# A decoder layer in fp32: a third weight pair by seven block products in the gate and up blocks, with the residual kept in DRAM meanwhile

## The chip, the cores and the metric

The kernel runs on one core of a Trainium2 chip. That core has a matmul engine (TensorE, PE), three engines for elementwise work (VectorE or DVE, ScalarE or ACT, GpSimd or POOL), a queue engine (SyncE, SP) that here issues almost all transfers, and 16 DMA engines. Engines run their instructions in order and wait for each other by semaphores.

The metric is the device time of one execution in microseconds (us), the median of several runs. Lower is better.

## The reference

One layer (DEPTH = 1) of a decoder over 256 tokens of 2048 features, all in float32:

```python
mem_n = rmsnorm(mem, mem_norm)
h = x
h = h + hybrid_mixer(rmsnorm(h, norm_mix), w_in, ..., w_out)
h = h + memory_cross_attention(rmsnorm(h, norm_xa), mem_n, w_q, w_k, w_v, w_o)
h = h + swiglu(rmsnorm(h, norm_ffn), w_gate, w_up, w_down)
return rmsnorm(h, norm_final)

def swiglu(h, w_gate, w_up, w_down):
    return (jax.nn.silu(h @ w_gate) * (h @ w_up)) @ w_down
```

The change touches the last step alone: `w_gate` and `w_up` are 2048 x 5632, `w_down` is 5632 x 2048. Mixer and attention stay as they are.

## The kernel before

**Products.** Every float32 operand of a large matmul is split into a high part that PE takes as it is (type `fp32r`) and the rest, a low part. A product is then three matmuls of 128 x 128 by 128 x 512 into one PSUM accumulator: high by high, low activations by high weights, high activations by low weights (`tok_mm`, lines 310, 311, 314). The stationary operand is a block of activations (128 features of 128 tokens), the moving one 512 columns of weights. For the 256 tokens there are two accumulators, called `tb` 0 and 1.

**Weights.** The weights come in one stream of tiles, 128 x 1024, each with two feature blocks of 512 columns (512 KB). `load_to` issues the loads on SP (line 197), up to six tiles ahead, into a pool `raw` of 6. `split_to` makes the high part on ACT (line 236, pool `hi` of 4) and the low part on DVE (line 237, pool `lo` of 4). A plain tile takes 12 matmuls: two feature blocks, two token blocks, three matmuls.

**Gate and up.** The stage runs in 11 blocks of 512 columns, `n` = 0 to 10. In each, gate (`g`) and up (`u`) have eight tiles, `c` = 0 to 7. Four PSUM accumulators (pool `acc` of 4) hold the block: gate and up by two token blocks.

**Seven products.** A gate tile and an up tile of the same features are, with the two token blocks and two feature blocks, a product of 2 x 2 blocks: eight block products the plain way, of three matmuls each, 24. In the blocks in `SEVEN` (1 to 8) the first two such pairs are computed by seven products instead (a Winograd form), 21 matmuls (`seven_mm`, lines 972 to 985). It needs:

- sums of weight blocks: `pair_sums` makes four sums of 128 x 512 on DVE (lines 211 to 214) when the pair's second tile is split, and splits three of them into high and low parts (ACT line 218, DVE line 219), in six tiles of the pool `slots` of 63;
- sums of activation blocks, once for the whole stage: `token_sums`, called in block 0, held in `tmp` tiles (8, all taken by two pairs) in `seven_a`;
- four more PSUM tiles (pool `msc` of 4), `shared[n]`, that collect products used in more than one result. After the block's last pair `p_post` (lines 936 to 940) makes four combinations of them, and `whole` (line 1207) adds one to each accumulator when it is read: for gate in `g_post`, for up in `u_post`.

**End of a block.** `u_post` multiplies gate and up (line 1224), transposes the result in 32 x 32 blocks (line 329), writes it to DRAM (`put`, line 342), reads it back with features on the partitions (`get`, line 349) and splits it into `gs` (lines 1234, 1235), two slots a feature pair, 44 by the end of the stage. The next block's matmuls need the up accumulators free.

**Down.** The down stage computes four blocks of 512 output columns, two at a time, with pairs by seven products too (`down_units`). It adds the residual `res` (8 slots of 128 x 512, loaded from x, updated by the mixer and the attention stage), which stays in SBUF all the while. `load_gain` loads `norm_final` ahead of some down tiles.

**Order.** The order on PE and SP is the order of the code (`manual_schedule`): `ffn_units` and `down_units` list the units, `unit` issues loads and splits ahead of the matmuls of its parts, and generators in `procs` (the `_post` functions) are moved on one step with each unit. On DVE and ACT a scheduler sets the order ahead of time; there is no choice at run time. Functions in `before` are called just before the load of a given weight tile is issued, so what they issue stands ahead of that load in SP's queue.

Of the kernel before, what the change touches and what calls it, by code (L numbers as in the profile page):

```python
# [17 lines left out]
F32 = mybir.dt.float32  # L18
F32R = mybir.dt.float32r
AF = mybir.ActivationFunctionType  # L20
ALU = mybir.AluOpType
# [3 lines left out]
T = 256  # L25
# [2 lines left out]
FF = 5632  # L28
FT = FF // 128
FN = FF // 512  # L30
SEVEN = range(1, 9)
OUT_GAPS = (2, 5, 4, 5)
GAPS = (2, 4, 5, 4, 5, 4)
H = 32
# [38 lines left out]
def ffn_units():  # L73


    o = [[((m, 0, c),)] for h in range(2) for m in "gu" for c in range(4 * h, 4 * h + 4)]
    for n in range(1, FN):
        if n in SEVEN:
            for q, rest in ((0, "g2 g3 g4 u2 u3 u4"), (1, "g5 g6 g7 u5 u6 u7")):
                o.append([(("g", n, q), ("u", n, q))])  # L80
                k = [(a[0], n, int(a[1])) for a in rest.split()]
                o += [[(a,), (b,)] for a, b in zip(k[0::2], k[1::2])]
        else:
            o += [[((m, n, c),), ((m, n, c + 1),)] for m in "gu" for c in range(0, KT // 2, 2)]
    return o
# [34 lines left out]
def stream_plan():  # L120

    p = [(("a0",), 512), (("b0",), 512)]
    p += [(("ab", kt), 1024) for kt in range(1, KT)]
    for n in range(2, 22):
        p += [(("in", n, c), 1024) for c in range(KT // 2)]
    p += [(("wo", n, c), 1024) for n, c in out_order()]
    p += [(k, 1024) for k in order_of(out_units())]
    p += [((m, c), 1024) for m in "kqv" for c in range(KT // 2)]
    p += [(("o", n, c), 1024) for n in range(4) for c in range(2)]
    p += [(k, 1024) for k in order_of(ffn_units() + down_units())]  # L130
    return p


def trunk(tc, wst, vecs, xp, xtp, mp, mtp, wdt_in, nfin, outp):
    nc = tc.nc
    plan = stream_plan()
    index = {k: i for i, (k, _) in enumerate(plan)}
    offs, o = [], 0
# [5 lines left out]
    with ExitStack() as ctx:  # L144
# [12 lines left out]
        drp = E(tc.tile_pool(name="scr", bufs=1, space=DRAM))  # L157
# [5 lines left out]
        def nm(s):  # L163
            cnt[0] += 1
            return f"{s}{cnt[0]}"

        def slot(shape=(128, 512), dt=F32):
            return sp.tile(list(shape), dt, tag="s", name=nm("s"))
# [4 lines left out]
        def acc():  # L173
            return accp.tile([128, 512], F32, tag="a", name=nm("a"))
# [6 lines left out]
        tt = nc.vector.tensor_tensor  # L181
# [87 lines left out]
        def small(name):  # L269
            return cp.tile([128, 2], F32, tag=name, name=nm(name), bufs=4)  # L270
# [15 lines left out]
        def inv_rms(e, n):  # L286
            r = small("rr")
            with tc.high_priority():
                ts(e, e, 1.0 / n, EPS, ALU.mult, ALU.add)
                gtt(r, e, half[:, 0:2], op=ALU.pow)  # L290
            return r
# [63 lines left out]
        procs = []  # L355
# [68 lines left out]
        def ahead_of(i, f):  # L424
            before.setdefault(i, []).append(f)
# [437 lines left out]
        res = [[None] * 4 for _ in range(2)]  # L863
# [9 lines left out]
        def add_to_res(n, accs, sums):  # L873

            for tb in range(2):
                h = res[tb][n]
                tt(h, accs[tb], h, ALU.add)
                j = gtp.tile([128, 512], F32, tag="g", name=nm("j"))
                act(j, h, AF.Square, accum_out=sums[:, tb, n:n + 1])
# [11 lines left out]
        def wait(k):  # L891
            for _ in range(k):
                yield

        def to_features(n, gain, dst, steps=(1, 1, 1)):

            if steps is None:
                for i in range(2):  # L900
                    ps = msc()
                    for f in (2 * i, 2 * i + 1):
                        for tb in range(2):
                            nc.tensor.transpose(ps[:, (f % 2) * T + tb * 128:(f % 2) * T + tb * 128 + 128],
                                                res[tb][n][:, f * 128:f * 128 + 128], ident)
                    for f in (2 * i, 2 * i + 1):
                        dst[4 * n + f] = gained(ps[:, (f % 2) * T:(f % 2) * T + T], gain, 4 * n + f)
                return
            t = turn_blocks([res[tb][n] for tb in range(2)])
            yield from wait(steps[0])  # L910
            w = put(t)
            yield from wait(steps[1])
            d = get(w)
            yield from wait(steps[2])
            for f in range(4):
                dst[4 * n + f] = gained(d[:, f], gain, 4 * n + f)

        def token_scale(name, sums, factor=None):

            e = small("rv")  # L920
            with tc.high_priority():
                nc.vector.tensor_reduce(e, sums, axis=mybir.AxisListType.X, op=ALU.add)
            r = inv_rms(e, D)
            out = cp.tile([128, 2], F32, name=name)
            ts(out, r, 1.0 if factor is None else factor, None, ALU.mult)
            return out


        shared, seven_a = {}, {}
# [19 lines left out]
            return  # L949
            yield  # L950

        def token_sums(key, parts):


            xy = fp.tile([128, 1024], F32, tag="f", name=nm("f"))
            w = 512 // len(parts)
            for i, (hi, lo) in enumerate(parts):
                tt(xy[:, i * w:i * w + w], hi.bitcast(F32), lo.bitcast(F32), ALU.add)
            a11, a21, a12, a22, *o = [xy[:, i * 128:i * 128 + 128] for i in range(8)]
            tt(o[0], a21, a22, ALU.subtract)  # L960
            tt(o[1], a11, o[0], ALU.subtract)
            tt(o[2], a21, a11, ALU.subtract)
            tt(o[3], a12, o[1], ALU.subtract)
            seven_a[key] = []
            for i in range(2):
                h, l = [tp.tile([128, T], F32R, tag="t", name=nm("t")) for _ in range(2)]
                y = xy[:, 512 + i * T:512 + i * T + T]
                nc.scalar.copy(h, y)
                tt(l, y, h.bitcast(F32), ALU.subtract)
                seven_a[key] += [(h[:, j * 128:j * 128 + 128], l[:, j * 128:j * 128 + 128]) for j in range(2)]  # L970
# [71 lines left out]
        for i, parts in enumerate(units_o):  # L1042
            for j in (i, i + 1, i + 2):
                if j < len(units_o) and len(units_o[j][0]) == 2 and units_o[j][0][0] not in seven_a:
                    c = units_o[j][0][0][2]
# [6 lines left out]
            _, n, c = keys[0]  # L1052
# [90 lines left out]
        h2g = {}  # L1143
        h2s = cp.tile([128, 2, 4], F32, name="h2s")
        ff = {}

        def o_post(n, accs):
            add_to_res(n, accs, h2s)
            if n == 3:
                ff["r"] = token_scale("fscale", h2s)  # L1150
            if n == 0:
                yield
            yield from to_features(n, "nffn", h2g, None if n == 0 else (4, 1, 0) if n == 1 else (6, 2, 1))
# [23 lines left out]
        with tc.high_priority():  # L1177
            for mb in range(2):
                Vs.append(slot())
                c = scales["mem"][:, mb:mb + 1]  # L1180
# [21 lines left out]
        def whole(m, n, tb, ps):  # L1202

            if n not in SEVEN:
                return ps
# [34 lines left out]
        def part_mm(part):  # L1240
            m, n, c = part[0]
            if len(part) == 2:
                g, u, p = faccs["g", n], faccs["u", n], shared[n]
                seven_mm(part, side_blocks(h2g, 2 * c), seven_a[c], g, u, p,
                         p + [g[0], g[1], u[0]] if c == 0 else [], p if c == 1 else [])
                return
            start = c == 0
            if n in SEVEN:
                start = (1,) if (m, c) == ("u", 2) else False
            tok_mm(faccs[m, n], part[0], side_blocks(h2g, 2 * c), (0, 1), start, c == KT // 2 - 1)  # L1250

        for i, parts in enumerate(ffn_units()):
            if i == len(ffn_units()) - 3:
                token_sums(("d", 0, 0), [gs[0]])
            if i == 8:
                for c in range(2):
                    token_sums(c, [(h2g[2 * c + k][:, 0:T], h2g[2 * c + k][:, T:]) for k in range(2)])
            post = []
            for part in parts:
                m, n, c = part[0]  # L1260
                for k in part:
                    if k[2] == 0:
                        faccs[k[:2]] = [acc(), acc()]
                if len(part) == 2:
                    if c == 0:
                        shared[n] = [msc() for _ in range(4)]
                    else:
                        post.append(p_post(n, shared[n]))
                elif c == KT // 2 - 1:
                    post.append((g_post if m == "g" else u_post)(n, faccs[m, n]))  # L1270
            unit([(list(part), lambda part=part: part_mm(part)) for part in parts], post or None)
# [123 lines left out]
        for i, parts in enumerate(units):  # L1395
# [7 lines left out]
            if len(parts[0]) == 2:  # L1403
                _, n, c = keys[0]
# [4 lines left out]
            n = keys[-1][1]  # L1409
# [136 lines left out]
```

## Time and profile before

| | |
|---|---|
| median of 3 runs | 1488.6 us (1488.46 to 1488.66) |
| span of the profiled execution, first to last instruction | 1487.0 us |
| DMA packets' bytes | 346.71 MB, mean 233 GB/s |
| weight loads (line 197) | 535 of 512 KB, 4.6 us from issue to landing |
| `put` and `get` | 42 each, 512 KB, 3.3 and 4.9 us |
| low parts of weights on DVE (line 237) | 539, 650.7 us busy |
| high parts of weights on ACT (line 236) | 539, 562.2 us busy |
| low parts of the weight sums (line 219) | 96, 65.0 us busy |

The page gives busy time by engine, then the chain of work that ended last: from the last instruction back, at each step to what released it. An engine that is busy all the time and holds that chain sets the time. A wait of another engine costs nothing by itself. In rows of instructions "out<-in" are the program's tile names without their numbers: `r` raw weights, `h` and `l` their parts, `b` and `f` sums, `s` slots, `a` and `m` PSUM tiles, `g` gate results. The busy time of an engine that overlaps its own instructions is the union of them, so the mean of one can be longer than the distance of two.

### The profile page before, as it was taken

Reading aid. Unit: us, or ns where it says so; the run is one execution under the profiler, and the core shown is the slowest. Engines: PE = TensorE matmul, PEld = TensorE weight load, DVE = VectorE, ACT = ScalarE, POOL = GpSimd, SP = SyncE. Lnnn points to the kernel's source line nnn. Section 1 sums busy time; section 2 is a strip of 40 time slices with the busy share of each in tenths; the row PEclk is TensorE's granted clock in tenths of the full one; section 3 lists DMA queues with packets and bytes.
Section 4 is the critical chain, followed back from the end, with each engine's and each line's share of the span. In section 5 each row is a group of like instructions: output and inputs, shape, how many; then the busy total and the mean of one; then the engine's idle time right before and its main releaser. Section 6 shows DMA issues by size and latency. Waiting matters only on the chain.

```text
span 1487.0 us, 18685 instructions
## 1 busy us (share of the span) xinstructions
PE 1476.3 (99%) x6637; PEld 1216.9 (82%) x6637; DVE 1138.9 (77%) x1596; ACT 837.1 (56%) x1176; POOL 33.8 (2%) x46
## 2 busy tenths in 40 slices
PE   9999999999999999999999999999999999999997
PEld 7788888888888888888888888888888888888886
DVE  6677777776785775997577888888887667979975
ACT  7576654867654554665465555555554444655553
POOL 0001000101000000000000000000000000000000
PEclk9999999999999999999999999999999999999999
DMA  9886766868767675768747676665667665765553
GB/s 361 275 282 227 268 225 219 289 225 308 235 214 278 212 233 198 267 228 283 265 159 237 234 248 212 231 213 206 232 226 245 223 225 198 240 215 196 201 189 108
DMA packets 149214, 346.71 MB, mean 233 GB/s; under 512 B 11360, under 2 KB 62976, under 8 KB 149120
## 3 DMA queue, kind: packets, MB, share of 16 engines
q1 hardware_dynamic: 140064, 338.64, 65.6%
q10 hardware_dynamic: 9056, 6.87, 1.5%
q8 instruction: 52, 0.85, 0.2%
q14 instruction: 42, 0.34, 0.1%
HBM read 321.30 MB, written 24.17 MB: 232 GB/s over the span
## 4 chain that ended last, share of the span: by engine, by line
PE 98%; DMA 0%; issue 0%; SPq 0%; ACT 0%; DVE 0%; DVEq 0%; POOLq 0%; POOL 0%
PE a L310 28%; PE a L311 28%; PE a L314 28%; PE m L985 2%; PE m L983 2%; PE m L982 2%; PE a L982 1%; PE a L985 1%; PE a L983 1%; PE m L731 1%; PE m L314 0%; PE m L310 0%; PE m L311 0%; DMA r<-in_w_dram 0%; PE m L1139 0%
## 5 line engine op out<-in xcount | busy, mean ns | idle before, releaser
L237 DVE TENSOR_TENSOR l<-r,h 128x1024 fp32r<-128x1024 f32 (+1 forms) x539 | 650.7, 1215 | 231.3 <-ACT h L236 220.3
L236 ACT CAST h<-r 128x1024 fp32r<-128x1024 f32 (+1 forms) x539 | 562.2, 1047 | 468.4 <-PE a L311 310.2
L310 PE MATMUL a<-h,s 128*128 128x512 f32 x1855 | 726.3, 392 | 0.4 <-ACT h L236 0.4
L311 PE MATMUL a<-h,s 128*128 128x512 f32 x1855 | 722.5, 389 | 0.0
L314 PE MATMUL a<-l,s 128*128 128x512 f32 x1855 | 498.9, 389 | 0.0
L310 PEld LDWEIGHTS a<-h,s 128*128 128x128 f32 x1855 | 348.5, 188 | 74.7 <-issue 2.0
L314 PEld LDWEIGHTS a<-l,s 128*128 128x128 f32 x1855 | 348.4, 188 | 72.5
L311 PEld LDWEIGHTS a<-h,s 128*128 128x128 f32 x1855 | 348.6, 188 | 71.5
L218 ACT CAST s<-b 128x512 fp32r<-128x512 f32 x64 | 38.7, 616 | 23.5 <-DVE b L211 19.8
L329 DVE STREAM_TRANSPOSE b<-s 128x512 f32<-128x512 f32 x62 | 40.7, 689 | 6.4 <-ACT s L336 6.4
L219 DVE TENSOR_TENSOR s<-b,s 128x512 fp32r<-128x512 f32 x64 | 43.2, 683 | 0.0
L672 DVE SCALAR_TENSOR_TENSOR t<-t,vec,t 128x255 f32<-128x255 f32 (+2 forms) x72 | 33.1, 490 | 3.9 <-ACT t L669 3.2
L211 DVE TENSOR_TENSOR b<-r,r 128x512 f32<-128x512 f32 x32 | 21.9, 685 | 14.3 <-DMA r<-in_w_dram 14.2
L336 ACT ACTIVATE s<-a,xr 128x512 f32<-128x512 f32 x42 | 26.4, 679 | 3.6 <-PE a L314 3.6
L1207 DVE TENSOR_TENSOR f<-a,f 128x512 f32<-128x512 f32 x32 | 20.5, 683 | 8.5 <-PE a L314 8.4
L985 PE MATMUL m<-s,t 128*128 128x512 f32 x64 | 24.9, 389 | 0.0
L982 PE MATMUL m<-s,t 128*128 128x512 f32 x64 | 24.9, 389 | 0.0
L983 PE MATMUL m<-s,t 128*128 128x512 f32 x64 | 24.9, 389 | 0.0
L218 ACT CAST s<-r 128x512 fp32r<-128x512 f32 x32 | 19.8, 617 | 6.0 <-DVE r L214 5.9
L212 DVE TENSOR_TENSOR r<-r 128x512 f32<-128x512 f32 x32 | 22.0, 686 | 0.4
L1234 ACT CAST s<-f 128x512 fp32r<-128x512 f32 x22 | 13.5, 619 | 15.4 <-DMA f<-w 15.4
L219 DVE TENSOR_TENSOR s<-r,s 128x512 fp32r<-128x512 f32 x32 | 21.8, 683 | 0.4 <-ACT s L218 0.4
(232 smaller groups left out, 1058.2 us busy)
## 6 DMA issues: line engine op xcount, KB each, us to landing
r<-in_w_dram SPq DMA_DIRECT2D x535, 512.0 KB, 4.6
w<-b SPq DMA_DIRECT2D x42, 512.0 KB, 3.3
f<-w SPq DMA_DIRECT2D x42, 512.0 KB, 4.9
s<-acsT ACTq DMA_DIRECT2D x24, 256.0 KB, 5.3
s<-in_xt_dram SPq DMA_DIRECT2D x16, 256.0 KB, 6.6
s<-in_mt_dram SPq DMA_DIRECT2D x8, 256.0 KB, 6.1
s<-in_m_dram SPq DMA_DIRECT2D x8, 256.0 KB, 5.9
s<-in_x_dram SPq DMA_DIRECT2D x7, 256.0 KB, 7.4
```

The source lines that it names most:

```text
L218: nc.scalar.copy(h, x)
L219: tt(l, x, h.bitcast(F32), ALU.subtract)
L236: nc.scalar.copy(h[:, c], r[:, c])
L237: tt(l[:, c], r[:, c], h[:, c].bitcast(F32), ALU.subtract)
L310: mm(ps[tb], ah, h[:, w], start=first and i == ks[0], stop=False)
L311: mm(ps[tb], al, h[:, w], start=False, stop=False)
L314: mm(ps[tb], blocks(i, tb)[0], l[:, i * 512:i * 512 + 512], start=False, stop=stop and i == ks[-1])
L329: nc.vector.transpose(t[:, tb * 512:tb * 512 + 512], src[tb])
L672: stt(a[:, d:], u[:, 0:T - d], v("cw", 4 * ct + k), a[:, d:], ALU.mult, ALU.add)
L982: mm(ps, ah, bh, start=any(ps is q for q in start), stop=False)
L983: mm(ps, al, bh, start=False, stop=False)
L985: mm(ps, ah, bl, start=False, stop=any(ps is q for q in stop))
```

## The change

In blocks 1 to 9 three pairs go by seven products, in block 10 two; before it was two in blocks 1 to 8. With three pairs the tiles stand in the order pair, `g3 g4 u3`, pair, `g5 u4 g6`, pair, `g7 u5 u6 u7`. The third pair's token sums take two slots instead of `tmp` tiles. The residual is written to DRAM in block 0 (`park`), its eight slots are free in between, and it is read back (`unpark`) ahead of the down tiles ("d", 0, 10) to ("d", 0, 17).

```diff
-SEVEN = range(1, 9)
+SEVEN = {n: 3 if n < 10 else 2 for n in range(1, 11)}
...
         if n in SEVEN:
-            for q, rest in ((0, "g2 g3 g4 u2 u3 u4"), (1, "g5 g6 g7 u5 u6 u7")):
+            plan = {2: ("g2 g3 g4 u2 u3 u4", "g5 g6 g7 u5 u6 u7"),
+                    3: ("g3 g4 u3", "g5 u4 g6", "g7 u5 u6 u7")}[SEVEN[n]]
+            for q, rest in enumerate(plan):
                 o.append([(("g", n, q), ("u", n, q))])
                 k = [(a[0], n, int(a[1])) for a in rest.split()]
-                o += [[(a,), (b,)] for a, b in zip(k[0::2], k[1::2])]
+                o += [[(a,) for a in k[i:i + 2]] for i in range(0, len(k), 2)]
...
-        def token_sums(key, parts):
+        def token_sums(key, parts, wide=False):
...
+            if wide:
+                h, l = slot(dt=F32R), slot(dt=F32R)
+                nc.scalar.copy(h, xy[:, 512:])
+                tt(l, xy[:, 512:], h.bitcast(F32), ALU.subtract)
+                seven_a[key] = [(h[:, j * 128:j * 128 + 128], l[:, j * 128:j * 128 + 128]) for j in range(4)]
+                return
...
+        parked = drp.tile([2, 4, 128, 512], F32, name="parked")
+
+        def park(n):
+
+            yield from wait(12)
+            for tb in range(2):
+                nc.sync.dma_start(parked[tb, n], res[tb][n])
+                yield
+
+        def unpark(tb, n):
+            res[tb][n] = slot()
+            nc.sync.dma_start(res[tb][n], parked[tb, n])
+
+        for n in range(4):
+            for tb in range(2):
+                ahead_of(index[("d", 0, 10 + 2 * n + tb)], lambda tb=tb, n=n: unpark(tb, n))
...
+            procs.append(park(n))
...
-                         p + [g[0], g[1], u[0]] if c == 0 else [], p if c == 1 else [])
+                         p + [g[0], g[1], u[0]] if c == 0 else [], p if c == SEVEN[n] - 1 else [])
...
-                start = (1,) if (m, c) == ("u", 2) else False
+                start = (1,) if (m, c) == ("u", SEVEN[n]) else False
...
-                for c in range(2):
-                    token_sums(c, [(h2g[2 * c + k][:, 0:T], h2g[2 * c + k][:, T:]) for k in range(2)])
+                for c in range(3):
+                    token_sums(c, [(h2g[2 * c + k][:, 0:T], h2g[2 * c + k][:, T:]) for k in range(2)], c == 2)
...
-                    else:
+                    elif c == SEVEN[n] - 1:
                         post.append(p_post(n, shared[n]))
```

Lines of the changed kernel are 2 higher up to 953, and 25 higher from the gate and up stage on: 237 becomes 239, 211 to 214 become 213 to 216, 219 becomes 221, 937 becomes 939, 1207 becomes 1232, 1224 becomes 1249, 1235 becomes 1260.

The order on DVE just after the end of block 1, before: it begins with the last transpose of `u_post`; then come the splits of plain tiles (237) and the sums of block 2's second pair (211 to 214), with the two splits of the returned result (1235) between them.

```order
L329 STREAM_TRANSPOSE b_7867<-g_7790 128x512
L237 TENSOR_TENSOR l_7875<-r_7773,h_7874 128x1024
L237 TENSOR_TENSOR l_7897<-r_7830,h_7896 128x1024
L237 TENSOR_TENSOR l_7901<-r_7840,h_7900 128x1024
L237 TENSOR_TENSOR l_7935<-r_7878,h_7934 128x1024
L211 TENSOR_TENSOR b_7982<-r_7916,r_7918 128x512
L237 TENSOR_TENSOR l_7939<-r_7880,h_7938 128x1024
L212 TENSOR_TENSOR r_7918<-r_7918 128x512
L1235 TENSOR_TENSOR s_7971<-f_7932,s_7970 128x512
L213 TENSOR_TENSOR b_7982<-b_7982,r_7918 128x512
L237 TENSOR_TENSOR l_7979<-r_7916,h_7978 128x1024
L1235 TENSOR_TENSOR s_7975<-f_7932,s_7974 128x512
```

And in the changed kernel, from the same transpose:

```order
L331 STREAM_TRANSPOSE b_7901<-g_7824 128x512
L239 TENSOR_TENSOR l_7909<-r_7807,h_7908 128x1024
L239 TENSOR_TENSOR l_7931<-r_7864,h_7930 128x1024
L239 TENSOR_TENSOR l_7935<-r_7874,h_7934 128x1024
L213 TENSOR_TENSOR b_7966<-r_7874,r_7912 128x512
L214 TENSOR_TENSOR r_7912<-r_7912 128x512
L215 TENSOR_TENSOR b_7966<-b_7966,r_7912 128x512
L221 TENSOR_TENSOR s_7972<-b_7966,s_7971 128x512
L216 TENSOR_TENSOR r_7874<-b_7966,r_7874 128x512
L221 TENSOR_TENSOR s_7976<-b_7966,s_7975 128x512
L239 TENSOR_TENSOR l_7984<-r_7912,h_7983 128x1024
L221 TENSOR_TENSOR s_7980<-r_7874,s_7979 128x512
```

The second pair's sums now follow two plain splits and the split of the pair's own first tile, and their splits (221) follow at once; the returned result's splits come after them.

The order on DVE at the end of block 10 and the start of the down stage, before: `u_post` of block 10 (1224, 329), then the sums and splits of the first down pair.

```order
L1224 SCALAR_TENSOR_TENSOR g_10801<-a_10785,fscale,g_10801 128x512
L1224 SCALAR_TENSOR_TENSOR g_10803<-a_10786,fscale,g_10803 128x512
L329 STREAM_TRANSPOSE b_10972<-g_10801 128x512
L329 STREAM_TRANSPOSE b_10972<-g_10803 128x512
L211 TENSOR_TENSOR b_10979<-r_10911,r_10913 128x512
L212 TENSOR_TENSOR r_10913<-r_10913 128x512
L213 TENSOR_TENSOR b_10979<-b_10979,r_10913 128x512
L219 TENSOR_TENSOR s_10985<-b_10979,s_10984 128x512
L214 TENSOR_TENSOR r_10911<-b_10979,r_10911 128x512
L219 TENSOR_TENSOR s_10989<-b_10979,s_10988 128x512
L237 TENSOR_TENSOR l_10997<-r_10913,h_10996 128x1024
L219 TENSOR_TENSOR s_10993<-r_10911,s_10992 128x512
```

And in the changed kernel:

```order
L1232 TENSOR_TENSOR f_11073<-a_10828,f_11073 128x512
L1232 TENSOR_TENSOR f_11073<-a_10829,f_11073 128x512
L1249 SCALAR_TENSOR_TENSOR g_11151<-f_11073,fscale,g_11151 128x512
L1249 SCALAR_TENSOR_TENSOR g_11154<-f_11073,fscale,g_11154 128x512
L331 STREAM_TRANSPOSE b_11204<-g_11151 128x512
L331 STREAM_TRANSPOSE b_11204<-g_11154 128x512
L213 TENSOR_TENSOR b_11211<-r_11135,r_11137 128x512
L214 TENSOR_TENSOR r_11137<-r_11137 128x512
L215 TENSOR_TENSOR b_11211<-b_11211,r_11137 128x512
L221 TENSOR_TENSOR s_11217<-b_11211,s_11216 128x512
L216 TENSOR_TENSOR r_11135<-b_11211,r_11135 128x512
L221 TENSOR_TENSOR s_11221<-b_11211,s_11220 128x512
```

The two corrections of the up accumulators (1232) are new there, ahead of the same rows, so that these rows end two places short: the split of the pair's second tile, next to last in the rows before, is the row that follows.

SP's queue around block 10's `put` and `get` (342, 349), before: loads of down tiles (197) and of `norm_final` (1281).

```order
L1281 DMA s_10954<-in_nfin_dram 128x512
L197 DMA r_10956<-in_w_dram 128x1024
L197 DMA r_11012<-in_w_dram 128x1024
L1281 DMA s_11020<-in_nfin_dram 128x512
L197 DMA r_11022<-in_w_dram 128x1024
L342 DMA w_11045<-b_10972 128x2x512
L197 DMA r_11055<-in_w_dram 128x1024
L197 DMA r_11071<-in_w_dram 128x1024
L349 DMA f_11085<-w_11045 128x8x128
```

And in the changed kernel, where these lines are 344, 351, 199 and 1306:

```order
L1306 DMA s_11184<-in_nfin_dram 128x512
L199 DMA r_11186<-in_w_dram 128x1024
L1165 DMA s_11244<-parked 128x512
L199 DMA r_11246<-in_w_dram 128x1024
L1165 DMA s_11254<-parked 128x512
L1306 DMA s_11256<-in_nfin_dram 128x512
L199 DMA r_11258<-in_w_dram 128x1024
L344 DMA w_11281<-b_11204 128x2x512
L199 DMA r_11291<-in_w_dram 128x1024
L199 DMA r_11307<-in_w_dram 128x1024
L351 DMA f_11321<-w_11281 128x8x128
```

Two loads of the parked residual (1165) now stand ahead of down tiles there; the other six follow in the same way behind the `get`.

## The prediction

> **What bounds the kernel now.** I read the page first, then busy time by windows, groups of instructions, waits, and the order of time in one gate/up block. Line numbers are those of the kernel before.
>
> ```profile
> span 1487.0 us, 18685 instructions
> PE 1476.3 (99%) x6637; PEld 1216.9 (82%) x6637; DVE 1138.9 (77%) x1596; ACT 837.1 (56%) x1176; POOL 33.8 (2%) x46
> PE 98%; DMA 0%; issue 0%; SPq 0%; ACT 0%; DVE 0%; DVEq 0%; POOLq 0%; POOL 0%
> ```
>
> TensorE (PE) is busy 1476.3 of 1487.0 us and holds 98% of the chain that ended last. So time goes where matmuls go, as long as no other engine makes PE wait. The runs' median is 1488.6 us, so 1.6 us lie around the span; I add them to every result below.
>
> ```profile
> 920.00:960.00 40.00, 40.00 (x178) 33.15 (x177) 33.90 (x43) 21.50 (x26) 0.00 (x0) 1.00 0.62 216
> 1160.00:1200.00 40.00, 40.00 (x178) 33.15 (x177) 23.16 (x23) 17.36 (x19) 0.00 (x0) 1.00 0.65 224
> 1240.00:1280.00 40.00, 40.00 (x178) 33.06 (x177) 35.45 (x55) 21.18 (x27) 0.00 (x0) 1.00 0.69 230
> 1360.00:1400.00 40.00, 40.00 (x178) 33.15 (x177) 38.88 (x67) 24.22 (x34) 0.00 (x0) 1.00 0.56 188
> ```
>
> Columns: length, then PE, PEld, DVE, ACT, POOL busy, granted clock, DMA share, GB/s. PE has no gap in any of these and its clock is 1.00. VectorE (DVE) is busy 33.90 of 40 us in blocks with two pairs (first row), 23.16 in plain blocks (second), and once 38.88 of 40, in the down stage, with PE still full. ScalarE is half idle everywhere. The next engine that could bind is therefore DVE, and only in the gate/up blocks that the change loads further.
>
> **What the change removes.** The period of a two-pair block stands between two equal places of the program, the up evacuations of neighbouring blocks:
>
> ```profile
> 907.01 1.29 DVE L1207 TENSOR_TENSOR f<-a,f 128x512 f32<-128x512 f32 x2 [1.04 <-PE a L314]
> 908.22 1.40 DVE L1224 SCALAR_TENSOR_TENSOR g<-f,fscale,g 128x512 f32<-128x512 f32 x2
> 909.54 1.30 DVE L329 STREAM_TRANSPOSE b<-g 128x512 f32<-128x512 f32 x2
> 910.76 3.45 DVE L237 TENSOR_TENSOR l<-r,h 128x1024 fp32r<-128x1024 f32 x3
> 917.10 0.69 DVE L211 TENSOR_TENSOR b<-r,r 128x512 f32<-128x512 f32 x1 [0.98 <-DMA r<-in_w_dram]
> 918.85 0.68 DVE L212 TENSOR_TENSOR r<-r 128x512 f32<-128x512 f32 x1
> 919.45 0.68 DVE L1235 TENSOR_TENSOR s<-f,s 128x512 fp32r<-128x512 f32 x1
> 920.05 0.68 DVE L213 TENSOR_TENSOR b<-b,r 128x512 f32<-128x512 f32 x1
> 920.65 1.22 DVE L237 TENSOR_TENSOR l<-r,h 128x1024 fp32r<-128x1024 f32 x1
> 921.79 0.68 DVE L1235 TENSOR_TENSOR s<-f,s 128x512 fp32r<-128x512 f32 x1
> 949.17 1.29 DVE L1207 TENSOR_TENSOR f<-a,f 128x512 f32<-128x512 f32 x2 [1.05 <-PE a L314]
> ```
>
> 949.17 - 907.01 = 42.16 us for 12 plain tiles of 12 matmuls and 2 pairs of 21, 186 in all: 0.2267 us a matmul. (A matmul's own 0.39 us overlaps its neighbours and is no price.) A pair of tiles costs 21 matmuls by the seven products and 24 plain, so each new pair takes 3 x 0.2267 = 0.68 us off PE. There are 16 pairs before (8 blocks x 2) and 29 after (9 x 3 + 2), 13 more, and 39 matmuls fewer, as PE's order has it (6433 rows, then 6394). **The gain on PE is 39 x 0.2267 = 8.84 us.** A three-pair block takes 183 x 0.2267 = 41.48 us on PE.
>
> **What it adds to DVE.** Each new pair needs four sums (L211 to L214) and three splits (L219); blocks 9 and 10 also get the four combinations of L937 to L940 and the four corrections of L1207.
>
> ```profile
> L237 DVE TENSOR_TENSOR l<-r,h 128x1024 fp32r<-128x1024 f32 x229 | 276.6, 1217 | 70.8 <-ACT h L236 70.5
> L219 DVE TENSOR_TENSOR s<-b,s 128x512 fp32r<-128x512 f32 x50 | 33.6, 683 | 0.0
> L1207 DVE TENSOR_TENSOR f<-a,f 128x512 f32<-128x512 f32 x32 | 20.5, 683 | 8.5 <-PE a L314 8.4
> L937 DVE TENSOR_TENSOR f<-m,f 128x512 f32<-128x512 f32 x9 | 6.2, 690 | 8.9 <-PE m L985 8.9
> ```
>
> The mean of one is 0.68 us, but the starts show what it occupies: 918.85, 919.45, 920.05, 920.65 are 0.60 apart, and a 1024-wide split takes 1.14 (920.65 to 921.79). I price by starts. A three-pair block holds 16 splits x 1.14 = 18.2, 21 pair operations x 0.60 = 12.6, eight of L937 to L940 and L1207 x 0.605 = 4.8 (907.01 to 908.22 for two), two of L1224 1.32, two transposes 1.22, two of L1235 1.2, and some 0.5 where a sum must wait for the one just ahead: **39.9 us of DVE against 41.48 us of PE**, 96%. That fits only if the waits inside the block shrink to 1.6 us.
>
> ```profile
> DVE l L237 <- ACT h L236: 20.1, 36, 0.9
> DVE b L211 <- DMA r<-in_w_dram: 10.5, 9, 1.6
> DVE f L937 <- PE m L985: 7.8, 7, 1.1
> DVE f L1207 <- PE a L314: 6.3, 6, 1.0
> ```
>
> These are the waits of 310 us (7.4 blocks; total, times, longest). Three of the four are DVE being early: for PE's accumulators (L937, L1207), and for a ScalarE cast that itself waits until PE frees one of four `hi` tiles. They vanish when DVE is later. The fourth, a pair's second weight tile still under way, is 1.4 us a block. In the order before, that load stands behind the store of the previous block in SP's queue; in the new one the loads of the second pair stand ahead of the store, and only the next block's first pair is exposed: its load goes out when the third pair's tiles are split, and DVE has just three splits (3.4 us) to do until it needs it.
>
> ```profile
> r<-in_w_dram SPq DMA_DIRECT2D x114, 512.0 KB, 4.3
> ```
>
> With 4.3 us to land, DVE idles about 1 us there, but the next thing in its queue waits for PE's third pair anyway.
>
> So I walk through one block along DVE's order, from PE's first matmul of the block at 0. PE (2.72 us a plain tile, 4.76 a pair) starts the second pair at 12.9, the third at 25.8, and ends at 41.5. DVE: the previous block's up evacuation (907.01 to 910.76) to 3.75; three splits to 7.2; the second pair's sums and splits to 12.9, of which PE reads the last ones from 15.2; three splits and two of L1235 to 17.5; the third pair's to 24.1, read from 28.1; one split to 25.2. For the next one ScalarE must first cast into a `hi` tile that PE frees at 24.9 (cast done 26.0): DVE waits 0.85. Two splits to 29.0; two sums of the next first pair to 30.4, where PE's third pair has just ended; the combinations, the gate's corrections, the rest of that pair's sums and splits and two plain splits, back to back, to 41.7. The up evacuation thus starts 0.2 us after PE ended the block. What is late next is u's first accumulator: PE needs it 16 matmuls (3.6 us) into the block, DVE frees it after 0.2 + 0.7. **I take no PE stall in the nine blocks**; the other end is rival 1. Below nothing is excluded: the change takes nothing else off PE.
>
> **The change of stage.** Block 10 now has corrections, so two L1207 stand between PE's last up matmul and the sums of the first down pair. Before:
>
> ```profile
> 1247.01 1.41 DVE L1224 SCALAR_TENSOR_TENSOR g<-a,fscale,g 128x512 f32<-128x512 f32 x2 [1.09 <-PE a L314]
> 1249.56 0.65 DVE L211 TENSOR_TENSOR b<-r,r 128x512 f32<-128x512 f32 x1
> 1253.31 1.22 DVE L237 TENSOR_TENSOR l<-r,h 128x1024 fp32r<-128x1024 f32 x1
> 1254.52 0.39 PE L983 MATMUL m<-s,t 128*128 128x512 f32 x1
> 1254.75 0.40 PE L985 MATMUL m<-l,t 128*128 128x512 f32 x1
> ```
>
> DVE works from 1247.01 without a pause; the split that L985 at 1254.75 reads ends at 1254.53. There is no slack at all, so 2 x 0.605 = **1.2 us are a stall of PE**, once. The queue behind it (splits of the next plain tiles) has over 2 us in hand, so it isn't paid twice.
>
> **Parking and the rest.** Eight stores and eight loads of 256 KB join SP's queue.
>
> ```profile
> s<-in_xt_dram SPq DMA_DIRECT2D x16, 256.0 KB, 6.6
> GB/s 361 275 282 227 268 225 219 289 225 308 235 214 278 212 233 198 267 228 283 265 159 237 234 248 212 231 213 206 232 226 245 223 225 198 240 215 196 201 189 108
> ```
>
> The nearest row is the 256 KB loads at the start, 6.6 us to land. The eight loads back move 2.1 MB in the 40 us after block 10, where 230 GB/s move already (the window 1240:1280): 282 in all, under the 361 of the first slice. They wait for slots that PE frees in block 10 or in the first down pair, well before the weight loads behind them are due. I take nothing; the other end is rival 3. The extra token sums for the third pair (about 2 us of DVE, once, in block 0) and block 9's and 10's combinations lie where DVE has 17 us free in 40 (1160:1200), under PE.
>
> **Sum.** 1487.0 - 8.84 + 1.2 = 1479.4 us span, **1481.0 us** with the 1.6 around it.
>
> **Rivals.**
>
> 1. *Waits don't shrink enough.* DVE does 39.9 us of work and keeps 1.4 us for the weight tile and 0.6 for ScalarE: 41.9, 0.4 over PE, in nine blocks 3.8 us, less a reserve of about 1 us before PE feels it: 1484 us. For it: the margin is 4%. Against: 38.88 of 40 us in the down stage with PE full.
>
> 2. *DVE becomes the bound: slower.* If an operation holds DVE for its whole duration, a block is 16 x 1.217 + 21 x 0.683 + 8 x 0.685 + 2 x (0.744 + 0.685 + 0.686), the last three from the rows below, or 43.5 us. That is 2.0 over PE, 18 in nine blocks, less a reserve of 2: 1481.0 + 16 = **1497 us**. It decides from 41.48 us a block, 1.6 over the price by starts: 0.03 us more for each of the 51 operations.
>
> ```profile
> L1224 DVE SCALAR_TENSOR_TENSOR g<-f,fscale,g 128x512 f32<-128x512 f32 x16 | 11.2, 744 | 0.0
> L329 DVE STREAM_TRANSPOSE b<-g 128x512 f32<-128x512 f32 x22 | 14.3, 685 | 0.0
> L1235 DVE TENSOR_TENSOR s<-f,s 128x512 fp32r<-128x512 f32 x22 | 15.0, 686 | 1.8 <-PE a L314 0.9 <-ACT s L1234 0.8
> ```
>
> Against it are the starts 0.60 apart, under the 0.68 of one. The Trainium skill speaks for it: "VectorE: DVE Perf Modes", section Terms, says that the pipeline is flushed after each operation and the next can't issue until it is empty; its section on the TRN2 errata gives (N+151)/0.96, 691 ns for N = 512, which fits the trace's 683 as a duration. By that rule the sum is this rival's; the trace's starts disagree with it as an issue interval.
>
> 3. *The loads back cost what was gained.* If no bandwidth were to spare, 2.1 MB at 230 GB/s delay the down weights by 9 us. Weight tiles are loaded six ahead (6 x 2.72 - 4.3 = 12 us in hand), which would hide it; but a pair's sums need both tiles early. If that leaves 2 us, the cost is 7: 1488 us. The first slice's 361 GB/s speak against it.
>
> That the change doesn't do what it says is excluded by the count of matmuls.
>
> **How the numbers follow.** Forecast 0.68 (from 1479.5, just under the PE sum without the stall, to 1482.5), rival 1 0.14, rival 3 0.08, rival 2 0.10. The range reaches through rival 1: 1479.5 to 1486.0, which leaves out 0.18. A measurement tells about 0.2%, 3 us, from no change: faster (under 1485.6) 0.80, same 0.10, slower 0.10.
>
> **What would show it.** After the change the windows of the gate/up stage show PE 40.00 of 40 with DVE near 38.5; the block period between up evacuations is 41.5 us (42 or more means rival 1, 43.5 rival 2); "L1207 <- PE" waits fall to near nothing; one PE gap of about 1.2 us stands where the first down pair waits for its split; SP shows no long wait at the loads back. PE idle in the middle of the stage, released by DVE, would prove me wrong.

## The result and the profile after

The changed kernel takes **1480.8 us** (median of 4 runs, 1480.44 to 1482.02) against 1488.6 us before: ratio 0.995, 95% interval 0.9936 to 0.9964. That is 7.8 us or 0.5% faster, and the interval does not reach 1. The page of the changed kernel:

```profile
span 1478.7 us, 18815 instructions
PE 1467.5 (99%) x6598; PEld 1209.3 (82%) x6598; DVE 1200.5 (81%) x1710; ACT 858.1 (58%) x1218; POOL 35.8 (2%) x46
PE 98%; DVE 1%; issue 0%; DMA 0%; SPq 0%; ACT 0%; DVEq 0%; POOLq 0%; POOL 0%
```

PE has 39 matmuls fewer (6637 to 6598), DVE 61.6 us more work, and PE still holds 98% of the chain. In busy time by windows of 40 us (length, then PE, PEld, DVE, ACT, POOL, granted clock, DMA share, GB/s) the two gate/up windows of before and the change of stage (the last row) now read:

```profile
920.00:960.00 40.00, 40.00 (x178) 33.14 (x177) 38.98 (x52) 23.05 (x30) 0.00 (x0) 1.00 0.65 233
1160.00:1200.00 40.00, 40.00 (x178) 33.10 (x178) 38.03 (x50) 23.20 (x30) 0.00 (x0) 1.00 0.66 228
1240.00:1280.00 40.00, 39.13 (x173) 32.06 (x173) 39.86 (x65) 23.74 (x32) 0.00 (x0) 1.00 0.71 253
```

DVE is busy 38 to 39 of 40 us and PE shows no hole in the first two windows. The last one has the only hole: 39.13 of 40. The waits of the stage, DVE's in the same 310 us for which the prediction gave them before (total, times, longest):

```profile
DVE l L239 <- ACT h L238: 11.6, 20, 1.5
DVE b L213 <- DMA r<-in_w_dram: 1.4, 2, 0.8
DVE f L1232 <- PE a L316: 0.4, 1, 0.4
```

13.4 us in place of 44.7. All the waits of PE in the whole run are two rows, the first of them at the start as before:

```profile
PE m L446 <- POOL U L442: 1.8, 1, 1.8
PE m L993 <- DVE l L239: 0.9, 1, 0.9
```

The second is the one at the first down pair. In order of time, PE and then DVE there:

```profile
1245.27 0.39 PE L991 MATMUL m<-s,t 128*128 128x512 f32 x1
1246.53 0.50 PE L993 MATMUL m<-l,t 128*128 128x512 f32 x1 [0.87 <-DVE l L239]
1246.86 0.40 PE L993 MATMUL m<-s,t 128*128 128x512 f32 x1
...
1237.76 1.29 DVE L1232 TENSOR_TENSOR f<-a,f 128x512 f32<-128x512 f32 x2 [1.05 <-PE a L316]
1241.51 0.65 DVE L213 TENSOR_TENSOR b<-r,r 128x512 f32<-128x512 f32 x1
1245.25 1.22 DVE L239 TENSOR_TENSOR l<-r,h 128x1024 fp32r<-128x1024 f32 x1
```

DVE works from 1237.76 without a pause to the end of the split at 1246.47, and PE starts the matmul that reads it at 1246.53. By starts PE loses 1.26 - 0.23 = 1.03 us there and 0.34 - 0.23 = 0.11 at the next matmul: 1.14 us.

### The profile page after: what moved, and what is told of

Its sections match the earlier page's. It is cut to its first block, busy times and chain, and to the rows that moved or that the text cites. A ratio compares the mean times of both kernels' runs of the same rounds, so it can differ in the third digit from the quotient of the medians.

```text
span 1478.7 us, 18815 instructions
## 1 busy us (share of the span) xinstructions
PE 1467.5 (99%) x6598; PEld 1209.3 (82%) x6598; DVE 1200.5 (81%) x1710; ACT 858.1 (58%) x1218; POOL 35.8 (2%) x46
## 4 chain that ended last, share of the span: by engine, by line
PE 98%; DVE 1%; issue 0%; DMA 0%; SPq 0%; ACT 0%; DVEq 0%; POOLq 0%; POOL 0%
PE a L312 27%; PE a L313 27%; PE a L316 27%; PE m L993 3%; PE m L990 3%; PE m L991 3%; PE a L991 2%; PE a L990 2%; PE a L993 2%; PE m L733 1%; PE m L316 0%; PE m L313 0%; PE m L312 0%; DMA r<-in_w_dram 0%; PE m L1147 0%
## 5 line engine op out<-in xcount | busy, mean ns | idle before, releaser
L312 PE MATMUL a<-h,s 128*128 128x512 f32 x1751 | 685.7, 392 | 0.1
L313 PE MATMUL a<-h,s 128*128 128x512 f32 x1751 | 681.9, 389 | 0.0
L316 PE MATMUL a<-l,s 128*128 128x512 f32 x1751 | 471.1, 389 | 0.0
L312 PEld LDWEIGHTS a<-h,s 128*128 128x128 f32 x1751 | 329.0, 188 | 70.5 <-issue 2.0
L316 PEld LDWEIGHTS a<-l,s 128*128 128x128 f32 x1751 | 328.7, 188 | 68.5
L313 PEld LDWEIGHTS a<-h,s 128*128 128x128 f32 x1751 | 329.0, 188 | 67.4
L220 ACT CAST s<-b 128x512 fp32r<-128x512 f32 x90 | 55.4, 617 | 54.4 <-DVE b L213 52.3
L221 DVE TENSOR_TENSOR s<-b,s 128x512 fp32r<-128x512 f32 x90 | 61.7, 685 | 0.0
L214 DVE TENSOR_TENSOR r<-r 128x512 f32<-128x512 f32 x45 | 30.9, 688 | 0.8
L216 DVE TENSOR_TENSOR r<-b,r 128x512 f32<-128x512 f32 x45 | 30.8, 684 | 0.2
L221 DVE TENSOR_TENSOR s<-r,s 128x512 fp32r<-128x512 f32 x45 | 30.8, 684 | 0.0
L215 DVE TENSOR_TENSOR b<-b,r 128x512 f32<-128x512 f32 x45 | 30.7, 683 | 0.0
L993 PE MATMUL m<-s,t 128*128 128x512 f32 x72 | 28.0, 389 | 0.0
L991 PE MATMUL m<-s,t 128*128 128x512 f32 x72 | 28.0, 389 | 0.0
L990 PE MATMUL m<-s,t 128*128 128x512 f32 x72 | 28.0, 389 | 0.0
```

The costliest lines, as they stand in the source:

```text
L220: nc.scalar.copy(h, x)
L221: tt(l, x, h.bitcast(F32), ALU.subtract)
L312: mm(ps[tb], ah, h[:, w], start=first and i == ks[0], stop=False)
L313: mm(ps[tb], al, h[:, w], start=False, stop=False)
L316: mm(ps[tb], blocks(i, tb)[0], l[:, i * 512:i * 512 + 512], start=False, stop=stop and i == ks[-1])
L990: mm(ps, ah, bh, start=any(ps is q for q in start), stop=False)
```

## The experiments

Ten kernels ran. Each time stands beside runs of the kernel before on the same chip (1488.3 to 1488.5 us).

| kernel | median, us | ratio to before, 95% interval | expected, us |
|---|---|---|---|
| park_alone | 1488.4 | 0.9998 (0.9989 to 1.0007) | 1488.6 |
| two_pairs | 1487.0 | 0.999 (0.9982 to 0.9999) | 1487.0 |
| plain10 | 1481.1 | 0.995 (0.9938 to 0.9961) | 1481.1 |
| late_pair | 1479.8 | 0.994 (0.9927 to 0.9953) | 1479.7 |
| best | 1479.1 | 0.9937 (0.9925 to 0.995) | 1479.1 |
| dve1 | 1484.1 | 0.997 (0.9959 to 0.9982) | 1480.8 to 1482 |
| dve2 | 1503.7 | 1.0102 (1.0088 to 1.0116) | 1495 |
| four_pairs | 1502.2 | 1.0091 (1.0076 to 1.0106) | 1501 |
| free1 | 1481.5 | 0.9955 (0.9941 to 0.9969) | 1480.8 to 1481.6 |
| free2 | 1497.5 | 1.0061 (1.0048 to 1.0073) | 1497 |

### Parking alone

```diff
-SEVEN = {n: 3 if n < 10 else 2 for n in range(1, 11)}
+SEVEN = {n: 2 for n in range(1, 9)}
...
-                for c in range(3):
+                for c in range(2):
                     token_sums(c, ...
```

> Pairs as before the change (two in blocks 1 to 8), with the residual still parked in DRAM and loaded back. Theory (parking costs nothing): the time of the kernel before, 1488.6 us, within 0.5, and no PE gap over 0.2 us from the gate and up stage on. Rival (the loads back delay the down weights): 1 to 7 us more, as PE gaps in the 40 us after block 10, with DVE or ACT waiting there for weight loads.

The time is that of before within the interval. The waits of PE in the whole run:

```profile
PE m L446 <- POOL U L442: 1.8, 1, 1.8
PE a L312 <- ACT h L238: 1.0, 1, 1.0
```

Both lie in the first 10 us of the program, on the first weights. No wait of PE is left where the residual comes back, so **parking is hidden** and rival 3 falls. In the changed kernel the transfers (the page's DMA issues: number, size, us to landing) and the longest of SP's waits at the loads back (L1165) read:

```profile
parked<-s SPq DMA_DIRECT2D x8, 256.0 KB, 8.0
s<-parked SPq DMA_DIRECT2D x8, 256.0 KB, 6.9
```

```profile
SPq L1165 <- DMA f<-w: 1.2, 1, 1.2
```

The loads land after 6.9 us, near the 6.6 that the prediction took from the first ones of the program, and SP hardly stops at them: its three other waits at L1165 are 0.2 or 0.3 us.

### Two pairs in blocks 1 to 10

```diff
-SEVEN = {n: 3 if n < 10 else 2 for n in range(1, 11)}
+SEVEN = {n: 2 for n in range(1, 11)}
...
-                for c in range(3):
+                for c in range(2):
                     token_sums(c, ...
```

> Two pairs in blocks 1 to 10, no third pair, parking kept: 20 pairs, 12 matmuls fewer than before. Theory (0.2267 us a matmul, and a stall of 1.1 us because block 10 has corrections now): 1488.6 - 2.72 + 1.1 = 1487.0 us, with one PE gap of about 1.1 us at the first down pair. Rival (the stall comes with the third pairs, which leave DVE late): no gap, 1485.9 us.

It takes 1487.0 us, and the waits of PE hold the same row as in the changed kernel:

```profile
PE m L993 <- DVE l L239: 0.9, 1, 0.9
```

There is no third pair here, so the stall does not come from those. Common to both kernels are block 10's two pairs with their corrections, and the loads back; `park_alone` has the loads back too and no such wait.

### Block 10 plain

```diff
-SEVEN = {n: 3 if n < 10 else 2 for n in range(1, 11)}
+SEVEN = {n: 3 for n in range(1, 10)}
```

> Three pairs in blocks 1 to 9, block 10 plain: 27 pairs, 6 matmuls more than the changed kernel. Theory (the stall at the first down pair is the two corrections of block 10): the stall of 1.1 us goes and 6 x 0.2267 = 1.36 us of matmuls come: 1480.8 + 0.25 = 1481.1 us, no PE gap at the first down pair. Rival (the stall has another cause, such as the loads back on SP's queue): the gap stays and the time is 1482.2 us.

It takes 1481.1 us. Of PE's waits only those at the start of the program remain, the 1.8 us as before and

```profile
PE a L312 <- ACT h L238: 0.4, 1, 0.4
```

The loads back stand here as in the changed kernel, so the stall was not theirs. Of the 1.36 us that block 10's two pairs save on PE, its corrections give back 1.14: the change would have lost almost nothing without block 10.

### The first down pair later, and a third pair in block 10

`late_pair`:

```diff
-        for c, k in enumerate(GAPS):
+        for c, k in enumerate(((4,) if n == 0 else GAPS[:1]) + GAPS[1:]):
...
-            before.setdefault(index[("d", 0, 9 + 2 * n)], []).append(lambda n=n: load_gain(n))
+            before.setdefault(index[("d", 0, 10 + 2 * n)], []).append(lambda n=n: load_gain(n))
```

> The changed kernel with the first down pair two plain tiles later (a gap of four tiles in place of two; the loads of norm_final move one tile later with it). Theory (the split that PE waits for is 1.1 us late, and two tiles give 5.4 us): the gap goes, 1480.8 - 1.1 = 1479.7 us. Rival (DVE or the loads are behind by more, and the stall only moves): a PE gap of 0.5 us or more remains somewhere in the first 40 us of the down stage, 1480.3 us or more.

`best` has, besides this:

```diff
-SEVEN = {n: 3 if n < 10 else 2 for n in range(1, 11)}
+SEVEN = {n: 3 for n in range(1, 11)}
```

> late_pair with a third pair in block 10 too: 30 pairs, 3 matmuls fewer. Theory: 3 x 0.2267 = 0.68 us less than late_pair, 1479.1 us, no PE gap. Rival (DVE is too late at the end of block 10 for a third pair there): a PE gap around the first down pair, 1479.8 us or more.

Besides the 1.8 us at the start PE waits once in the whole run of `best`, at the start too:

```profile
PE a L312 <- ACT h L238: 0.2, 1, 0.2
```

The stall is gone in both (`late_pair` waits for the same cast at the start, 0.9 us, and nowhere else). The times fall by 1.0 and a further 0.7 us, as worked out; the ratio's intervals overlap with that of the changed kernel, so it is the missing row that shows the gain, and the times agree with it. `late_pair` moves the loads of `norm_final` as well; that the stall was theirs is excluded by `plain10`, which has them in the old place and no stall. `best` is the fastest of all that ran: 1479.1 us.

### More work for DVE

`dve1` does the first sum of every gate/up pair twice, `dve2` three times; what is computed stays the same.

```diff
-            tt(f[:, a], g[:, a], u[:, a], ALU.add)
+            for _ in range(2 if key[0] == "g" else 1):
+                tt(f[:, a], g[:, a], u[:, a], ALU.add)
```

> The changed kernel with the first sum of each gate/up pair done twice, the same result: 3 more DVE operations of 128x512 in a block of blocks 1 to 9 (2 in block 10). Theory (an operation holds DVE for 0.60 us; DVE's waits of about 1.7 us a block are reserve): 3 x 0.60 = 1.8 us a block use the reserve up and no more: 1480.8 to 1482 us, with DVE's waits for ACT casts in the stage near zero. Rival (the operations take their whole 0.68 us, 2.05 us a block, and the waits are no reserve because they are set by PE): 9 x 1 us or more, 1489 us or more.

> The same with the first sum done three times: 6 more operations in a block. Theory (0.60 us each): 3.6 - 1.75 = 1.85 us a block over PE, 9 blocks 16.6 us, less 2 to 3 us of lead that PE can lose before it waits: 1480.8 + 14 = 1495 us, block period 43.3 us, PE waiting for DVE. Rival by durations (0.683 us each): 4.1 - 1.75 = 2.35 us a block, 21 - 2.5, 1499 us, block period 43.8 us. Rival (DVE has much more hidden slack): below 1485 us.

Both were slower than expected: 3.3 us over the changed kernel in place of 0 to 1.2, and 22.9 in place of 14. In order of time, one block of `dve2` from one `u_post` (L1250) to the next:

```profile
956.20 1.41 DVE L1250 SCALAR_TENSOR_TENSOR g<-f,fscale,g 128x512 f32<-128x512 f32 x2
...
963.25 2.14 DVE L214 TENSOR_TENSOR b<-r,r 128x512 f32<-128x512 f32 x3
965.42 0.69 DVE L215 TENSOR_TENSOR r<-r 128x512 f32<-128x512 f32 x1
966.03 0.69 DVE L216 TENSOR_TENSOR b<-b,r 128x512 f32<-128x512 f32 x1
...
1000.41 1.40 DVE L1250 SCALAR_TENSOR_TENSOR g<-f,fscale,g 128x512 f32<-128x512 f32 x2
```

The period is 44.21 us, and the three equal sums (x3) take 965.42 - 963.25 = 2.17, that is 0.72 each, where the next ones are 0.61 apart. In the program's order on DVE the repeated sum waits, by DVE's own semaphore, for the end of the one ahead, since both write the same place:

```
L214 TENSOR_TENSOR b_7974<-r_7882,r_7920 128x512 [waits DMAHW4_49]
L214 TENSOR_TENSOR b_7974<-r_7882,r_7920 128x512 [waits DVE_49] x2
L215 TENSOR_TENSOR r_7920<-r_7920 128x512 [waits DVE_49]
L216 TENSOR_TENSOR b_7974<-b_7974,r_7920 128x512
```

My expectation priced it like a sum without such a wait. At 0.72, DVE's work of a block without the extra is 44.21 - 6 x 0.72 = 39.9 us, and from `dve1`, whose period is 42.01, 42.01 - 3 x 0.72 = 39.85:

```profile
949.75 1.41 DVE L1250 SCALAR_TENSOR_TENSOR g<-f,fscale,g 128x512 f32<-128x512 f32 x2
991.76 1.41 DVE L1250 SCALAR_TENSOR_TENSOR g<-f,fscale,g 128x512 f32<-128x512 f32 x2
```

To test that reading, `free1` and `free2` add as many sums, which write the half that a later sum overwrites, so that neither has to wait for a sum just ahead. `free1` has the first of the two added places, `free2` both:

```diff
+            if key[0] == "g":
+                tt(f[:, b], g[:, a], u[:, a], ALU.add)
             tt(f[:, a], g[:, a], u[:, a], ALU.add)
+            if key[0] == "g":
+                tt(f[:, b], g[:, a], u[:, a], ALU.add)
```

> The changed kernel with 3 more DVE operations a block again, but none that must wait for the one just ahead: each gate/up pair's first sum is also written to the half of the same buffer that the third sum overwrites. Theory (in dve1 and dve2 the repeated sums stand 0.72 us apart because each waits for the end of the one ahead, which writes the same place; an operation without that wait takes 0.60): block period 39.86 + 1.8 = 41.66 us, 0.18 over PE, 9 x 0.18 = 1.6 us, about the lead that dve1 and dve2 showed: 1480.8 to 1481.6 us. Rival (an added operation costs 0.72 us whatever it is): as dve1, period 42.02, 1484.1 us.

> The same with two such operations for each pair, one ahead of the first sum and one behind it, 6 more a block. Theory: 39.86 + 3.6 = 43.46 us a block, 9 x 1.98 = 17.8 us, less a lead of 1.6: 1497 us. Rival (0.72 us each): as dve2, period 44.2, 1503.7 us. If only the second of the two, which writes the same place two operations later, waits for the end of the one ahead of it: 43.8 us, 1500 us.

Both times came out as the theory has them (1481.5 and 1497.5 us). `free2` in order of time; L214, L215 and L217 are the three sums, L218 the second sum of before:

```profile
954.01 1.40 DVE L1253 SCALAR_TENSOR_TENSOR g<-f,fscale,g 128x512 f32<-128x512 f32 x2
961.05 0.68 DVE L214 TENSOR_TENSOR b<-r,r 128x512 f32<-128x512 f32 x1
961.66 0.68 DVE L215 TENSOR_TENSOR b<-r,r 128x512 f32<-128x512 f32 x1
962.26 0.68 DVE L217 TENSOR_TENSOR b<-r,r 128x512 f32<-128x512 f32 x1
962.98 0.69 DVE L218 TENSOR_TENSOR r<-r 128x512 f32<-128x512 f32 x1
...
997.61 1.41 DVE L1253 SCALAR_TENSOR_TENSOR g<-f,fscale,g 128x512 f32<-128x512 f32 x2
```

0.61, 0.60 and then 0.72 apart: only the second sum, which overwrites what the one ahead still reads, waits. L217, which overwrites what L214 wrote two places ahead, still starts 0.60 after L215. Each of them lasts 0.68 or 0.69 all the same. The period is 43.60. A window of `free1`, and the first matmuls of two later blocks, show how far DVE can be filled:

```profile
920.00:960.00 40.00, 40.00 (x178) 33.12 (x177) 39.90 (x53) 22.18 (x29) 0.00 (x0) 1.00 0.64 226
```

```profile
988.16 0.39 PE L992 MATMUL m<-h,s 128*128 128x512 f32 x1
1029.79 0.39 PE L992 MATMUL m<-h,s 128*128 128x512 f32 x1
```

DVE is busy 39.90 of 40 and PE shows no hole. But the two blocks start 41.63 us apart, 0.15 over the 41.48 of PE's matmuls. PE loses that much a block there, spread so thin that neither its busy time nor its waits show it: a matmul lasts 0.39 us and the next starts 0.23 after it, so one that starts up to 0.16 us late leaves no hole.

### Four pairs

Built on `late_pair`, with the fourth pair's token sums in slots as the third's:

```diff
-SEVEN = {n: 3 if n < 10 else 2 for n in range(1, 11)}
+SEVEN = {n: 4 if n < 10 else 2 for n in range(1, 11)}
...
-                    3: ("g3 g4 u3", "g5 u4 g6", "g7 u5 u6 u7")}[SEVEN[n]]
+                    3: ("g3 g4 u3", "g5 u4 g6", "g7 u5 u6 u7"),
+                    4: ("g4 u4", "g5 u5", "g6 u6", "g7 u7")}[SEVEN[n]]
...
-                for c in range(3):
+                for c in range(4):
```

> late_pair with four pairs in blocks 1 to 9 (order: pair, g4 u4, pair, g5 u5, pair, g6 u6, pair, g7 u7): 27 matmuls fewer than late_pair, 6.1 us on PE, and 7 more DVE operations a block. Theory (DVE becomes the bound): DVE needs 39.9 + 7 x 0.60 = 44.1 us a block, PE 40.8; 9 blocks at 44.1 in place of 41.5 are 23.5 us more, less 2 to 3 of lead: 1479.8 + 21 = 1501 us. Rival (DVE is still not the bound, the gain goes on): 1473.7 us.

The row of `u_post` in neighbouring blocks, and the waits of PE but for the 1.8 us at the start:

```profile
957.27 1.41 DVE L1250 SCALAR_TENSOR_TENSOR g<-f,fscale,g 128x512 f32<-128x512 f32 x2
1001.33 1.40 DVE L1250 SCALAR_TENSOR_TENSOR g<-f,fscale,g 128x512 f32<-128x512 f32 x2
```

```profile
PE a L991 <- DVE f L1233: 13.6, 8, 1.7
PE m L994 <- DVE l L240: 6.9, 8, 0.9
PE a L313 <- ACT s L890: 1.4, 1, 1.4
PE a L314 <- DVE s L891: 0.6, 1, 0.6
```

DVE sets the period, 44.06 us, in place of 41.48, and PE, with 27 matmuls less to do, waits for it in eight of the nine blocks. The last two rows are of block 0, where the fourth pair's token sums get in the way. They cost about 4 us, as the last section works out, which the expectation did not have: that it came near the time is in part luck. The step after the third pair turns the gain into a loss of 22 us, some 18 of them by DVE.

## Why the prediction was right

**The matmuls.** 39 at 0.2267 us. The records of PE are 39 fewer, and the first matmuls of neighbouring three-pair blocks start 41.48 us apart, as predicted (41.47 in the second of these):

```profile
988.23 0.39 PE L990 MATMUL m<-h,s 128*128 128x512 f32 x1
1029.71 0.39 PE L990 MATMUL m<-h,s 128*128 128x512 f32 x1
1071.18 0.39 PE L990 MATMUL m<-h,s 128*128 128x512 f32 x1
```

The prediction wanted this judged by the distance of `u_post` rows, and gave 42 us or more to rival 1. That sign is not safe:

```profile
1031.12 1.40 DVE L1249 SCALAR_TENSOR_TENSOR g<-f,fscale,g 128x512 f32<-128x512 f32 x2
1073.49 1.40 DVE L1249 SCALAR_TENSOR_TENSOR g<-f,fscale,g 128x512 f32<-128x512 f32 x2
1114.07 1.40 DVE L1249 SCALAR_TENSOR_TENSOR g<-f,fscale,g 128x512 f32<-128x512 f32 x2
```

The distances are 42.37 and 40.58 us, while PE goes on at 41.48. In the first of the two blocks DVE waits 0.82 us for a pair's weight tile and is late at its end; in the second its waits for casts are 0.73 us in place of 1.55, and it has caught up.

The experiments on the number of pairs (two_pairs, plain10, best) follow the same price within 0.1 us.

**DVE's work.** Priced at 39.9 us a block by the starts of operations. Where DVE is the bound, the period is its work, and it can be read: 39.85 and 39.9 us (dve1, dve2), 44.06 - 7 x 0.60 = 39.86 (four_pairs), 41.63 - 1.8 = 39.83 (free1), 43.60 - 3.6 = 40.0 (free2). This was the decision that mattered. Rival 2 took the 0.68 us that an operation lasts and had 43.5 us a block; the Trainium skill's "VectorE: DVE Perf Modes", section Terms, speaks for that price, and these periods speak against it.

**The waits.** Predicted to shrink to 1.6 us a block; 13.4 us in 310 are 1.8. Which they are was partly off: the wait for a pair's second weight tile, put at about 1 us a block, came twice in 310 us (1.4 in all), and the one for ScalarE's cast, put at 0.85, is 11.6 in all, or 1.6 a block. The walk through the block held most of that without naming it: from the end of its one wait at 26.05 two splits at 1.14 end at 28.3, not at 29.0, and the profile has a second wait for a cast there (0.77 and 0.59 us in the block whose first matmul is the one at 988.23). In sum the waits are little smaller than rival 1 had them (1.8 a block against 2.0), but they are slack: `free1` cuts those for casts to 0.4 us in 375 and fills the time with sums, and PE then loses 0.15 us a block, not rival 1's 0.4. Rival 1 took them for a price and fell with that.

**The stall.** 1.2 us predicted at the first down pair, 1.14 found, at the matmul and the split that were named; two_pairs keeps it and plain10 loses it with block 10's corrections. Two small errors in it cancel. "No slack at all" was not quite so: before, the split ended 0.22 us ahead of its matmul (1254.53 and 1254.75), now 0.06 ahead, so 0.16 of the 1.2 us was absorbed. And 0.11 is lost at the next matmul, which the prediction didn't have.

**Parking.** Nothing predicted, nothing found (park_alone).

**The sum.** 1479.4 us of span predicted, 1478.7 found. Most of the difference isn't the change's: the profile of before holds a wait of 0.4 us for the first weight cast at the start of the program, as below, which the profile of after happens not to have. In park_alone it is 1.0, in best 0.2, so this spot alone moves a run by up to 1 us.

```profile
PE a L310 <- ACT h L236: 0.4, 1, 0.4
```

**What was wrong** came after the prediction: the expectations of dve1 and dve2. They missed the 0.12 us by which an operation waits for the one just ahead, and they put the lead that PE can lose in the stage at 2 to 3 us in dve2. Over the nine blocks DVE's periods there are 9 x (44.21 - 41.48) = 24.6 us too long and the time rose by 22.9, so PE is spared 1.7 in all; from dve1 it is 9 x (42.01 - 41.48) - 3.3 = 1.5.

## What to carry to other kernels

Where one engine is full and the change hands its work to another, price the second by the distance of the starts in the densest stretch that the trace has, not by the durations: here the one said 96% full and right, the other 105% and wrong. Then look for the places where its work has no slack at all, such as a change of stage, and move the work that is waited for away from them: two plain tiles put between gave back the 1.0 us. Doubling a cheap operation until the time rises tells how much room is left, if the added operation doesn't wait for the one just ahead. And where instructions overlap, a busy share of 100% doesn't show that an engine loses nothing: compare the distance of equal places in the program.

## What the runs showed of the hardware

**Waiting for oneself costs 0.12 us.** Sums of 128x512 on DVE that don't wait for the one just ahead start 0.60 us apart though each lasts 0.68; those that do wait start 0.72 apart (dve2 against free2). The Trainium skill's "VectorE: DVE Perf Modes", section "The DRAIN you can't avoid", says that a semaphore costs nothing extra, from eight `tensor_copy` operations that took as long with one after each as with one at the end; these two runs, which differ in six such waits a block, are 6.3 us apart.

**PE came back at half speed after two short holes.** In block 0 of `four_pairs` PE waited 1.39 us and, one matmul later, 0.58 us. In order of time, and then in windows (columns as above):

```profile
807.15 0.49 PE L313 MATMUL a<-h,s 128*128 128x512 f32 x1 [1.39 <-ACT s L890]
808.22 0.79 PE L314 MATMUL a<-h,s 128*128 128x512 f32 x1 [0.58 <-DVE s L891]
808.81 0.63 PE L313 MATMUL a<-h,s 128*128 128x512 f32 x1
809.24 0.63 PE L314 MATMUL a<-h,s 128*128 128x512 f32 x1
```

```profile
807.00:811.50 4.50, 3.77 (x9) 2.79 (x10) 3.49 (x7) 2.23 (x5) 0.00 (x0) 0.64 1.02 387
811.50:815.00 3.50, 3.50 (x17) 2.87 (x16) 1.23 (x1) 1.53 (x2) 0.00 (x0) 0.98 1.04 414
```

Matmuls start 0.43 us apart where 0.23 is the rule, and the granted clock is 0.64 over these 4.5 us and 0.98 right after. The single hole of 0.87 us in the changed kernel left it at 1.00, as did those of up to 0.9 us in `dve2` (clock 1.00 from 900 to 1200). From the four low-part matmuls at 804.68 to the matmul at 812.44 PE starts 16, which take 16 x 0.2267 = 3.63 us elsewhere and 7.76 here: 4.1 us lost. "TensorE: Matmul & The Clock Gate" of the Trainium skill, Part 1, puts the fall after an idle window of about 3.4 us; here 2 us in two pieces were enough. What else decides it was not tried.
